# A double step of the blocked down projection written as two single steps

## The chip, the cores and the metric

One core of one Trainium2 chip runs the kernel; the other seven are idle. The metric is the device time of one execution in microseconds (us), the median of several runs. The engines are named as in the profile: PE (matmul), PEld (weight load), DVE (vector), ACT (scalar), POOL (GpSimd), SP (the queue that issues most transfers).

## What is computed

One layer of a streaming encoder, 512 positions by 1024 features, float32. Three parts come one after the other: a mixer (gated short convolution beside attention), its output projection with a residual sum, and a channel mixer with 2816 hidden features. Only the channel mixer touches the change:

```python
h = rms_norm(x, norm_ffn_g[l])
up = causal_dwconv(h @ w_up[l], conv_ffn_w[l])
a, b = jnp.split(up, 2, axis=-1)
x = x + (jax.nn.silu(a) * b) @ w_down[l]
...
return rms_norm(x, norm_f_g)
```

`silu(a) * b` is called the gated product here. It has 22 blocks of 128 features, and `w_down` has 8 output blocks of 128.

## The kernel before

**Arithmetic.** Each float32 operand is held as a rounded high part and a remainder (`wh`, `wl` for weights, `gh`, `gl` for the gated product), and each product is three matmuls: `wh*gh`, `wh*gl`, `wl*gh`.

**Steps.** The hidden blocks are worked through in two phases (`PHASES`, blocks 0 to 11 and 12 to 21). In a phase every block `j` is first projected up, convolved and gated, and then the down projection of the phase runs as a list of steps (`STEPS[ph]`, line 48). The down projection works on pairs: `(i, q)` is output pair `i` (blocks 2i, 2i+1) by hidden pair `q` (blocks 2q, 2q+1), done with seven half-size products where eight would be usual. A step holds two such `(i, q)` (a double step) or one (a single step). In phase 1 output pairs 0, 1, 2 by hidden pairs 6 to 10 are done so, and blocks 6 and 7 of the output follow plainly (`dp` chunks, `pdA` and `pdB`).

**Chunks.** A step needs two weight chunks: P (3 blocks of 128 columns for each `(i, q)`) and F (4 blocks). A double step has a P of 768 and an F of 1024 columns, with 18 and 24 matmuls; a single step has 384 and 512 columns, with 9 and 12. `split()` (line 253) turns a raw chunk into `wh` (ACT, line 275) and `wl` (DVE, line 279). `wh` and `wl` have two buffers each, so the split of a chunk can begin when PE has done with the chunk two before it. The raw P and `dp` chunks have four buffers (tag `raw`), the raw F chunks four (`rf`), filled in order by SP (line 182, `load`).

**F chunks are made on the chip.** The weight sums of F are built in DRAM by `make_forms` (line 190), for groups of up to two steps of the same size: `put` copies from SP (line 208) and accumulating `add` transfers from POOL (line 211), six for each group in the order put, add, put, add, put, add, each waiting for the one before. They are issued at `slot()` calls, two for each block `j` and one for each P chunk of the down steps: operation `k` of group `g` at slot `3k+g` in phase 1 (`GROUPS[1]`). Slots 14, 16 and 18 stand ahead of blocks 19, 20 and 21, slots 15, 17 and 19 in the middle of them, and slot 20 at the first P chunk.

**Forms of the gated product.** For each hidden pair, `glu()` (line 1230) queues the sums and differences `t13` and `t24` (lines 1256 to 1261) and four high/low splits `hl` (ACT line 1265, then DVE line 1266): `ge`, then the parts x=0, x=4 and x=2 of `go`. They become `gh` and `gl` of the seven products. Products of P read `gh`/`gl` numbers 0 (from `ge`), 1 (x=0) and 6 (x=4), in this order; those of F read 2 (x=0), 3, 4 (x=2) and 5 (x=4).

**The list `later`.** Such work isn't issued at once. It waits in `later` with a chunk number from which it is due and an estimated time; each `split()` issues what is due and fits its budget (`run_later`, 1.6 us at a P chunk and 0.75 us at an F chunk in the down steps), behind the two instructions of the split. Whatever a P or F chunk needs and is still in the list is issued ahead of that chunk's matmuls (`flush`). For the last pair of a phase the forms are due from the fourth to the sixth chunk after the gating:

```python
d = (2, 3, 4) if j + 1 < PHASES[ph][1] else (4, 5, 6)
w = [(d[0], 0.85, t13), (d[0], 0.85, t24), (d[1], 0.7, hl(ge[:, : 1 + ph, :], slice(g0, g0 + 1 + NF * ph, NF)))]
w += [(d[x > 0 and 2 or 1], 0.7, hl(go[:, x : x + 2, :], slice(g0 + 1 + x, g0 + 3 + x))) for x in (0, 4, 2)]
```

The order of matmuls on PE is that of the program, and so are the orders of the transfers on SP and POOL and of the gating products on POOL. The instructions of ACT and DVE are ordered by a planner when the program is built, which takes the earliest in the program among those ready by its own model. `seven()` (line 824) runs the steps: flush, matmuls of the chunk, then the split of the next chunk. When an output pair has had its last step, `combine()` (line 1277) queues its sums.

Of the kernel before, what the change touches and what calls it, by code (L numbers as in the profile page):

```python
# [47 lines left out]
STEPS = (  # L48
    tuple(((i, q), (i, q + 1)) for i, q in ((0, 0), (0, 2), (1, 0), (1, 2), (0, 4), (1, 4)))
    + tuple(((i, q), (i, q + 1)) for i in (3, 2) for q in (0, 2, 4)),  # L50
    (((2, 6), (2, 7)), ((2, 8), (2, 9)), ((0, 6), (0, 7)), ((0, 8), (2, 10)), ((0, 9), (0, 10)))
    + (((1, 6),), ((1, 7), (1, 8)), ((1, 9), (1, 10))),
)

# [1485 lines left out]
```

## Time and profile before

| | |
|---|---|
| median of 3 runs | 695.39 us (695.22 to 695.82) |
| the profiled execution's own time | 695.33 us |
| its span, first to last instruction | 693.5 us |
| PE busy | 682.6 us (98%) |
| DVE busy | 554.8 us (80%) |
| ACT busy | 368.5 us (53%) |
| POOL busy | 190.6 us (27%) |
| mean granted PE clock | 0.998 |

The profile is of one execution. Its page lists the busy time of each engine, the chain of work that ended last, and groups of instructions. Further views are the waits (who waited for whom), the timeline (start, duration, engine, line and operation of each instruction, with the idle time before it in brackets), stretches of time with each engine's busy time and the granted clock, and the transfers with their time to landing. Successive matmuls overlap in the records, so the time of a chunk is the distance between the starts of its first matmul and the next chunk's first.

In phase 1 of this execution the down steps begin at about 630.5 us and the plain `dp` part at 668.3 us. The steps are numbered 0 to 7 here, with their chunks P0, F0, P1 and so on; step 3 is `((0, 8), (2, 10))`.

### The profile page before, as it was taken

The numbers are of one execution on the slowest core, as the hardware profiler recorded it, in microseconds if no ns is written. First come the engines' busy times: TensorE is split into PE (matmuls) and PEld (weight loads), VectorE is DVE, ScalarE is ACT, GpSimd is POOL, SyncE is SP. The second block draws the span as 40 slices with busy tenths as digits, with TensorE's granted clock in tenths as the row PEclk, the third lists the DMA queues.
The fourth block names the chain that finished last, engine by engine and source line by source line (L and its number), as shares of the span: only waits on it lengthen the run. The fifth ranks groups of instructions, "written<-read, shape, count | busy, mean of one in ns | idle before, by whom it ended". The sixth has DMA issues, their size and how long they took to land. (4 is left out here: it accounts for less than half of the span.)

```text
span 693.5 us, 14692 instructions
## 1 busy us (share of the span) xinstructions
PE 682.6 (98%) x5936; PEld 680.4 (98%) x5936; DVE 554.8 (80%) x858; ACT 368.5 (53%) x579; POOL 190.6 (27%) x201
## 2 busy tenths in 40 slices
PE   9999999999999999999999999999999999999995
PEld 8999999999999999999999999999999999999995
DVE  6677887877577778769778799998777889987794
ACT  5665765554554444546564555546454635545572
POOL 6134947542020201214400144340100415321000
PEclk9999999999999999999999999999999999999999
DMA  8618999552668586788997498888945996576313
GB/s 310 225 68 288 219 235 215 132 116 92 193 137 225 164 276 202 231 305 208 160 306 243 127 246 212 203 215 272 244 139 174 336 243 157 160 188 182 132 31 122
DMA packets 65012, 137.53 MB, mean 198 GB/s; under 512 B 5760, under 2 KB 30352, under 8 KB 64688
## 3 DMA queue, kind: packets, MB, share of 16 engines
q1 hardware_dynamic: 44664, 107.28, 46.4%
q0 software_dynamic: 18464, 26.03, 23.7%
q10 hardware_dynamic: 1816, 3.29, 1.3%
q8 instruction: 46, 0.75, 0.5%
q14 instruction: 22, 0.18, 0.1%
HBM read 132.31 MB, written 47.71 MB: 260 GB/s over the span
## 5 line engine op out<-in xcount | busy, mean ns | idle before, releaser
L211 POOL DMA_DIRECT2D f<-in_wst_dram x66 | 77.1, 1361 | 28.1 <-DMA f<-f 27.8
L309 PE MATMUL p_up<-x1l,wh_up 128*128 128x256 f32 x416 | 81.1, 276 | 0.0
L309 PE MATMUL p_up<-x1h,wh_up 128*128 128x256 f32 x416 | 81.1, 276 | 0.0
L309 PE MATMUL p_up<-x1h,wl_up 128*128 128x256 f32 x416 | 81.0, 276 | 0.0
L279 DVE TENSOR_TENSOR wl_F<-raw_F,wh_F 128x1024 fp32r<-128x1024 f32 (+1 forms) x42 | 55.9, 1332 | 20.7 <-ACT wh_F L275 20.6
L275 ACT ACTIVATE wh_F<-raw_F 128x1024 fp32r<-128x1024 f32 (+1 forms) x42 | 44.3, 1054 | 40.9 <-PE dn L327 26.9
L309 PEld LDWEIGHTS p_up<-x1l,wh_up 128*128 128x128 f32 x416 | 62.7, 188 | 0.0
L309 PEld LDWEIGHTS p_up<-x1h,wh_up 128*128 128x128 f32 x416 | 62.6, 188 | 0.0
L309 PEld LDWEIGHTS p_up<-x1h,wl_up 128*128 128x128 f32 x416 | 62.6, 188 | 0.0
L309 PE MATMUL p_in<-xgh,wh_in 128*128 128x256 f32 x288 | 56.8, 279 | 0.0
L309 PE MATMUL p_in<-xgh,wl_in 128*128 128x256 f32 x288 | 56.6, 278 | 0.0
L309 PE MATMUL p_in<-xgl,wh_in 128*128 128x256 f32 x288 | 56.5, 278 | 0.0
L279 DVE TENSOR_TENSOR wl_P<-raw_P,wh_P 128x768 fp32r<-128x768 f32 (+1 forms) x42 | 41.7, 993 | 14.6 <-ACT wh_P L275 8.9
L275 ACT ACTIVATE wh_P<-raw_P 128x768 fp32r<-128x768 f32 (+1 forms) x42 | 35.1, 835 | 32.1 <-PE dn L327 21.8
L327 PE MATMUL dn<-gh,wh_F 128*128 128x256 f32 x216 | 51.0, 276 | 0.0
L327 PE MATMUL dn<-gl,wh_F 128*128 128x256 f32 x216 | 51.0, 276 | 0.0
L1239 POOL TENSOR_TENSOR ge<-fu,fu 128x512 f32<-128x512 f32 x11 | 20.1, 1829 | 109.6 <-DVE fu L570 76.4
L279 DVE TENSOR_TENSOR wl_up<-raw_up,wh_up 128x1024 fp32r<-128x1024 f32 x34 | 43.8, 1289 | 7.4 <-ACT wh_up L275 7.4
L275 ACT ACTIVATE wh_up<-raw_up 128x1024 fp32r<-128x1024 f32 x34 | 35.9, 1054 | 18.4 <-PE p_up L309 8.3
L309 PEld LDWEIGHTS p_in<-xgh,wh_in 128*128 128x128 f32 x288 | 44.7, 188 | 0.7
L309 PEld LDWEIGHTS p_in<-xgl,wh_in 128*128 128x128 f32 x288 | 43.7, 188 | 0.0
L309 PEld LDWEIGHTS p_in<-xgh,wl_in 128*128 128x128 f32 x288 | 43.6, 188 | 0.0
(343 smaller groups left out, 2214.1 us busy)
## 6 DMA issues: line engine op xcount, KB each, us to landing
raw_F<-f SPq DMA_DIRECT2D x41, 512.0 KB, 5.9
raw_up<-in_wup_dram SPq DMA_DIRECT2D x34, 512.0 KB, 5.4
raw_P<-in_wst_dram SPq DMA_DIRECT2D x41, 384.0 KB, 5.4
raw_in<-in_win_dram SPq DMA_DIRECT2D x24, 512.0 KB, 3.6
f<-in_wst_dram POOLq DMA_DIRECT2D x41, 256.0 KB, 7.0
f<-in_wst_dram SPq DMA_DIRECT2D x20, 512.0 KB, 7.2
f<-in_wst_dram POOLq DMA_DIRECT2D x20, 512.0 KB, 9.2
f<-f SPq DMA_DIRECT2D x40, 256.0 KB, 6.6
```

The costliest lines, as they stand in the source:

```text
L211: return lambda: keep(nc.gpsimd.dma_start(dst, src, accum_op=ALU.add))
L275: ins = nc.scalar.activation(hi, raw, AF.Copy)
L279: ins = nc.vector.tensor_sub(lo, raw, hi.bitcast(F32))
L309: keep(nc.tensor.matmul(out[:, cs], w, x[:, cs], start=start and i == 0 and c == 0, stop=stop and i == 2 and c == len(cut) - 1,))
L327: keep(nc.tensor.matmul(out, wl if x == 1 else wh, xl if x == 2 else xh, start=opens and bk not in seen, stop=closes and bk not in left,))
L1239: keep(nc.gpsimd.tensor_mul(ge, a.rearrange(halves_of, h=2), b.rearrange(halves_of, h=2)))
```

## The change

Step 3 of phase 1 is replaced by two single steps, `(0, 8)` and then `(2, 10)`:

```diff
-    (((2, 6), (2, 7)), ((2, 8), (2, 9)), ((0, 6), (0, 7)), ((0, 8), (2, 10)), ((0, 9), (0, 10)))
+    (((2, 6), (2, 7)), ((2, 8), (2, 9)), ((0, 6), (0, 7)), ((0, 8),), ((2, 10),), ((0, 9), (0, 10)))
     + (((1, 6),), ((1, 7), (1, 8)), ((1, 9), (1, 10))),
```

The list has nine steps afterwards. The new steps are called 3a, `(0, 8)`, and 3b, `(2, 10)`, here, and the others keep their old numbers. All that is derived from the list follows: the order of the products, the chunks in `stream`, the layout of the weights in `_layout`, the groups of `make_forms` (five before: steps 0 and 1, 2 and 3, 4, 5, 6 and 7; six after: 0 and 1, 2, 3a and 3b, 4, 5, 6 and 7), and the points at which `later` is worked off.

## The prediction

> **What bounds the kernel now.** I read the page's head first, then PE's waits, then the timeline of PE around the longest of them, then DVE and ACT at the same place. The page says that PE is the bound: 682.6 of 693.5 us busy, so time is only to be had where PE stands still or where something else makes it stand still.
>
> ```profile
> span 693.5 us, 14692 instructions
> ...
> PE 682.6 (98%) x5936; PEld 680.4 (98%) x5936; DVE 554.8 (80%) x858; ACT 368.5 (53%) x579; POOL 190.6 (27%) x201
> ```
>
> Among PE's waits the longest single one is for a form of the gated product, on the line of the down steps (total, times, longest):
>
> ```profile
> PE dn L327 <- DVE gl L1266: 1.4, 1, 1.4
> ```
>
> PE's timeline places it in step 3, the step that the change divides. The rows below are the first matmuls of F2, P3, the two around the wait, and the first of P4, F4, P5, F5 and P6 (start, duration).
>
> ```profile
> 642.02 0.28 PE L327 MATMUL dn<-gh,wh_F 128*128 128x256 f32 x1
> ...
> 644.74 0.28 PE L327 MATMUL dn<-gh,wh_P 128*128 128x256 f32 x1
> ...
> 645.90 0.38 PE L327 MATMUL dn<-gh,wh_P 128*128 128x256 f32 x1
> 647.65 0.39 PE L327 MATMUL dn<-gl,wh_P 128*128 128x256 f32 x1 [1.36 <-DVE gl L1266]
> ...
> 651.40 0.28 PE L327 MATMUL dn<-gh,wh_P 128*128 128x256 f32 x1
> ...
> 653.52 0.28 PE L327 MATMUL dn<-gh,wh_F 128*128 128x256 f32 x1
> ...
> 656.24 0.28 PE L327 MATMUL dn<-gh,wh_P 128*128 128x256 f32 x1
> ...
> 657.26 0.28 PE L327 MATMUL dn<-gh,wh_F 128*128 128x256 f32 x1
> ...
> 658.62 0.35 PE L327 MATMUL dn<-gh,wh_P 128*128 128x256 f32 x1
> ```
>
> F2's 24 matmuls take 644.74 - 642.02 = 2.72 us, so one takes 0.1134 us when nothing holds it up. At that pace step 3 (42 matmuls) takes 4.76 us; it takes 651.40 - 644.74 = 6.66 us. The bracket shows 1.36 us of idle time, but the step loses 1.90 us: 1.64 us between the starts of the two matmuls at the wait (1.75 less 0.11), and 0.26 us after it, where the matmuls follow each other more slowly. P4 behind it is slow as well, 653.52 - 651.40 = 2.12 us where 18 matmuls at pace are 2.04, another 0.08 us. So up to 1.98 us, 0.28% of the time, hang on this place. It isn't the granted clock: that is 1.00 in this stretch (its last three columns are clock, transfer share and GB/s).
>
> ```profile
> 644.70:648.60 3.90, 2.54 (x21) 2.28 (x21) 2.89 (x4) 1.63 (x3) 0.00 (x0) 1.00 0.39 134
> ```
>
> What PE waits for can be followed on ACT and DVE. The matmul at 647.65 is the twelfth of P3. In the order of `passes` the first twelve are `wh*gh` and `wh*gl` of six products, first three of (0, 8), then three of (2, 10), and the twelfth reads `gl` number 6 of pair 10, part x=4.
>
> ```profile
> 643.75 0.63 ACT L1265 ACTIVATE gh<-go 128x512 fp32r<-128x512 f32 x1 [0.32 <-DVE go L1260]
> 644.28 1.05 ACT L275 ACTIVATE wh_F<-raw_F 128x1024 fp32r<-128x1024 f32 x1
> 645.24 0.61 ACT L1265 ACTIVATE gh<-go 128x512 fp32r<-128x512 f32 x1
> ```
>
> ```profile
> 642.42 0.96 DVE L279 TENSOR_TENSOR wl_P<-raw_P,wh_P 128x768 fp32r<-128x768 f32 x1 [0.15 <-ACT wh_P L275]
> 643.30 0.42 DVE L1260 SCALAR_TENSOR_TENSOR go<-go 128x256 f32<-128x256 f32 x1
> ...
> 645.77 1.22 DVE L279 TENSOR_TENSOR wl_F<-raw_F,wh_F 128x1024 fp32r<-128x1024 f32 x1
> 646.91 0.69 DVE L1266 TENSOR_TENSOR gl<-go,gh 128x512 fp32r<-128x512 f32 x1
> ```
>
> The reader is to see a queue, not one slow instruction: `flush` puts three high/low splits of pair 10 ahead of P3's matmuls, the last sums that they need (`t24`) are themselves only issued with the split of P3 (643.30), and the split of F3 gets in between on both engines (644.28 and 645.77). The last form is done at 646.91 + 0.69 = 647.60, and PE goes on at 647.65.
>
> **The change part by part.**
>
> *PE.* The same 42 matmuls, in another order: P3a 9, F3a 12, P3b 9, F3b 12. The trace has one single step, step 5: P5 takes 657.26 - 656.24 = 1.02 us and F5 658.62 - 657.26 = 1.36, together 2.38, half of a double step. So the matmuls cost nothing more, 2 x 2.38 = 4.76 us.
>
> *When pair 10 is needed.* P3a and F3a read pair 8 only, whose forms are long done. With P3a starting at 644.74 as before, F3a starts at 645.76, P3b at 647.12, F3b at 648.14 and P4 at 649.50. The sixth matmul of P3b is the one that reads x=4: due at 647.12 + 5 x 0.1134 = 647.69. That is 0.09 us after the form was done even in the old order of work (647.60).
>
> *When pair 10 is ready.* Budgets are now spread over more splits: `t24` and `ge` with P3a (as before), x=0 with F3a (0.7 us of 0.75), x=4 and x=2 with P3b (1.4 of 1.6). `flush` finds nothing left at P3b. The splits are smaller; step 5 has their durations, on ACT and then on DVE:
>
> ```profile
> 653.02 0.53 ACT L275 ACTIVATE wh_P<-raw_P 128x384 fp32r<-128x384 f32 x1 [1.03 <-PE dn L327]
> 655.54 0.64 ACT L275 ACTIVATE wh_F<-raw_F 128x512 fp32r<-128x512 f32 x1 [1.99 <-PE dn L327]
> ```
>
> ```profile
> 653.98 0.55 DVE L279 TENSOR_TENSOR wl_P<-raw_P,wh_P 128x384 fp32r<-128x384 f32 x1
> ...
> 656.50 0.69 DVE L279 TENSOR_TENSOR wl_F<-raw_F,wh_F 128x512 fp32r<-128x512 f32 x1 [0.77 <-ACT wh_F L275]
> ```
>
> Laid out by hand with these, without any overlap of neighbours, and with 0.62 and 0.69 us for the two halves of a form: on ACT `wh` of F3a ends at 644.64 (it can start when F2's 16th matmul ends, 644.00), x=0 at 645.26, `wh` of P3b at 646.12 (after P3a's sixth matmul, 645.59), x=4 at 646.74, x=2 at 647.36, `wh` of F3b at 648.00. On DVE `wl` of F3a runs from 644.91 (F2's end) to 645.60, x=0 to 646.28, `wl` of P3b to 646.83, **x=4 to 647.51** (due 647.69), x=2 to 648.19 (due at F3b's fourth matmul, 648.48), `wl` of F3b to 648.88 (due at its ninth, 649.04). `wh` of F3b has 0.14 us to spare, the others 0.16 to 0.29. So the wait goes, but narrowly, and DVE is what is late next.
>
> *Cost of the pieces.* DVE works 2 x 0.55 - 0.96 + 2 x 0.69 - 1.22 = 0.30 us more, ACT 2 x 0.53 - 0.85 + 2 x 0.64 - 1.05 = 0.44 us (0.85 is the row of `wh` of P0 below). Both are in the layout above, hidden behind PE. If that cover were gone, 0.30 us of DVE would come straight off the gain. The Trainium skill, "VectorE: DVE Perf Modes", section on the TRN2 errata, speaks against the change here: each DVE or ACT instruction on SBUF pays a fixed time whatever its length, so it asks for tiles of at least 512 elements, and 384 is below. The rows agree that halves cost more than half (0.55 against 0.96); by the rule alone the change would cost, and by the rows the cost lies under PE.
>
> *Transfers.* SP issues two more weight loads and three more `put`, POOL three more `add`, for the sixth group; the bytes are the same. They fall on slots that were empty: puts on 5, 11 and 17, adds on 8, 14 and 20. The one that can hold up others is the put of slot 17. It is queued on SP behind the last `raw_up` load and ahead of the load of P0, and waits for the add of slot 14, which on POOL stands at the latest behind `ge` of block 18. Behind it on SP are the loads of P0, F0 and all later chunks.
>
> ```profile
> 601.49 0.33 SPq L182 DMA_DIRECT2D raw_up<-in_wup_dram  x1
> 609.51 0.33 SPq L182 DMA_DIRECT2D raw_P<-in_wst_dram  x1
> ```
>
> ```profile
> 603.26 3.23 POOL L1239 TENSOR_TENSOR ge<-fu,fu 128x512 f32<-128x512 f32 x1 [6.08 <-DVE fu L570]
> 606.44 1.08 POOL L211 DMA_DIRECT2D f<-in_wst_dram  x1
> ```
>
> The adds between 534 and 640 us take this long to land, and so do the P loads in the same stretch; the third row is the split of P0 on ACT:
>
> ```profile
> DMA to landing us min/median/max: 4.7/7.0/12.3
> ```
>
> ```profile
> DMA to landing us min/median/max: 2.9/4.9/9.1
> ```
>
> ```profile
> 625.22 0.85 ACT L275 ACTIVATE wh_P<-raw_P 128x768 fp32r<-128x768 f32 x1 [0.83 <-PE p_up L309]
> ```
>
> So the new add starts at about 606.4 and lands at 613.4, at worst 618.7; P0's load starts 4 to 9 us later than its 609.51 and lands at 618.3, at worst 627.8. P0's matmuls start three double steps before P3, at 644.74 - 3 x 4.76 = 630.5, and need `wh` 0.85 us earlier to begin, by 629.6. The stall on SP stays hidden, at worst by 1.8 us. I take 0 for it. An add costs POOL 1.08 us, and POOL's next product, at 614.85, was idle before it for 7.32 us: hidden as well.
>
> *Behind the steps.* From P4 on each engine has the same instructions in the same order, 1.9 us earlier. One transfer there was just in time: the second `dp` load, whose split on ACT stands in front of the split of P6.
>
> ```profile
> 649.98 4.91 SPq L182 DMA_DIRECT2D raw_dp<-in_wdp_dram  x2
> ```
>
> ```profile
> DMA to landing us min/median/max: 2.6/2.6/2.6
> ```
>
> ```profile
> 657.17 0.64 ACT L275 ACTIVATE wx<-raw_dp 128x512 fp32r<-128x512 f32 x1 [0.99 <-DMA raw_dp<-in_wdp_dram]
> 657.71 0.83 ACT L275 ACTIVATE wh_P<-raw_P 128x768 fp32r<-128x768 f32 x1
> ```
>
> It was issued at about 654.6, landed 2.6 us later, and `wh` of P6 was ready at 658.54 for a first matmul at 658.62. Any longer landing is PE's loss one for one. Afterwards the loads ahead of it are closer: F7's follows the end of `wl` of F3b (648.88) instead of F3 (646.91 + 0.08), so it and the first `dp` load overlap. Bounds: below nothing (0.15 us back, if P6 were to run at pace), and 3.2 us, if it takes the 5.8 us that is the median of the F loads between 534 and 640 us:
>
> ```profile
> DMA to landing us min/median/max: 3.2/5.8/9.1
> ```
>
> I take 0.15 us lost, near the row of this very load, since the transfer engines are busy 0.19 of the time while it is under way (last column but one):
>
> ```profile
> 654.00:656.00 2.00, 2.00 (x20) 2.00 (x19) 1.73 (x4) 0.46 (x1) 0.00 (x0) 1.00 0.19 41
> ```
>
> *Sum.* The profiled execution took 695.33 us, 1.83 outside its span of 693.5; the median of the runs is 695.39, so the two agree within 0.06 and I work from the median. 695.39 - 1.98 + 0.15 = **693.6 us**, 0.26% less.
>
> **The rivals.** *A. The forms come late again.* If the planner lets the split of F3b pass in front of x=4, as it let F3 pass in front of it before (645.77), then `wl` of F3b ends at about 648.1 to 648.2, x=4 at 648.8, and P3b stands for 1.15 us, with 0.25 behind it. That gives 695.39 - 1.98 + 1.40 = 694.8. Against it: x=4 then has its sums done 2 us earlier, so it is ready when its turn comes. The skill's rule above leans to this side.
>
> *B. The second `dp` load is somewhat late.* With 3.5 us to landing instead of 2.6 PE loses 0.9 us: 695.39 - 1.98 + 0.9 = 694.3.
>
> *C. The same load is very late, and the kernel is slower.* Place: ACT's queue at the split of P6. From a landing of 2.6 + 2.0 = 4.6 us on nothing is gained, from 6.0 us on the loss passes 0.2%. At 7.5 us, between the median and the longest of the F loads, PE stands 4.9 us: 695.39 - 1.98 + 4.9 = 698.3. For it: ACT takes its queue in order, and loads in the busier stretch do take that long. Against it: only 256 KB, and few transfers beside it.
>
> **How the numbers follow.** A measurement of this kernel can tell about 0.2%, 1.4 us, from no change, so "faster" ends at 694.0. The forecast, 693.0 to 694.0, has 0.62; A 0.14; B 0.10; C 0.14, of which 0.10 beyond 6.0 us and 0.04 between, within 0.2%. Faster is 0.62, same 0.14 + 0.10 + 0.04 = 0.28, slower 0.10. The range takes in A and B with a margin of 0.2 us, so 693.0 to 695.0. Below it lies only the case that another stall of PE happens to go too.
>
> **What would show it.** Right: no wait of PE for `gl` on line 1266 in phase 1; P3a to P4 4.8 us apart; x=4 done before P3b's sixth matmul; everything behind 1.8 to 2.0 us earlier. Wrong: a wait in P3b for `gl` or in F3b for `wh_F` (A); a wait of PE for `wh_P` behind step 5, with ACT waiting for `raw_dp` for longer than 0.99 us (B, C); a wait at P0 for `wh_P`, with SP standing at line 208 beyond 619 us. The prediction fails altogether if the planner orders ACT and DVE differently far from step 3, which the trace of before can't show.

## The result, and the profile after

The kernel after takes 692.83 us (median of 7 runs, 692.54 to 694.68), the kernel before beside it 695.55 us (694.89 to 695.84). The ratio is 0.9967 with a 95% interval of 0.9955 to 0.9978: 0.33% faster, between 1.5 and 3.1 us; the two medians lie 2.7 us apart. The median lies 0.2 us below the lower end of the range. The profiled execution of after took 692.54 us, with a span of 690.8 us against 693.5.

PE's waits in the kernel after (total, times, longest): the wait on line 1266 is gone, and what is left is elsewhere and stands in before too.

```profile
PE warm L115 <- DVE ones L107: 1.1, 1, 1.1
PE p_up L327 <- DVE wl_up L279: 0.4, 1, 0.4
PE dn L327 <- DVE wl_F L279: 0.4, 1, 0.4
```

PE's timeline of after, with the first matmuls of P3a, F3a and P3b, the sixth of P3b, and the first of F3b, P4, F4, P6 and F6:

```profile
644.63 0.28 PE L327 MATMUL dn<-gh,wh_P 128*128 128x256 f32 x1
...
645.65 0.28 PE L327 MATMUL dn<-gh,wh_F 128*128 128x256 f32 x1
...
647.01 0.28 PE L327 MATMUL dn<-gh,wh_P 128*128 128x256 f32 x1
...
647.57 0.28 PE L327 MATMUL dn<-gl,wh_P 128*128 128x256 f32 x1
...
648.03 0.28 PE L327 MATMUL dn<-gh,wh_F 128*128 128x256 f32 x1
...
649.39 0.28 PE L327 MATMUL dn<-gh,wh_P 128*128 128x256 f32 x1
...
651.43 0.28 PE L327 MATMUL dn<-gh,wh_F 128*128 128x256 f32 x1
...
656.53 0.28 PE L327 MATMUL dn<-gh,wh_P 128*128 128x256 f32 x1
...
658.57 0.28 PE L327 MATMUL dn<-gh,wh_F 128*128 128x256 f32 x1
```

The reader is to see the four chunks at full pace, 649.39 - 644.63 = 4.76 us, with no bracket of idle time. On DVE the form that was late comes as the first of a row of two, behind `wl` of P3b and ahead of `wl` of F3b:

```profile
646.09 0.55 DVE L279 TENSOR_TENSOR wl_P<-raw_P,wh_P 128x384 fp32r<-128x384 f32 x1
646.59 1.30 DVE L1266 TENSOR_TENSOR gl<-go,gh 128x512 fp32r<-128x512 f32 x2
647.80 0.68 DVE L279 TENSOR_TENSOR wl_F<-raw_F,wh_F 128x512 fp32r<-128x512 f32 x1
```

x=4 is done at about 646.59 + 0.69 = 647.28, 0.29 us before the matmul that reads it. Counted from the start of step 3, the form was done at 2.86 us in before and is done at 2.65 us in after, while its reading, after 11 matmuls at pace, would have come at 1.25 us in before and comes at 2.94 us in after. So the reading moved by 1.69 us and the form by only 0.21 us: in the change itself nearly all of the gain is the later reading.

The 2.7 us between the two profiled executions divide so, from the starts of the same chunks in both and the last output transfer that SP issues (`dp` starts at 668.29 and 666.05):

| stretch | before | after | difference |
|---|---|---|---|
| start of the span to P3 | 644.74 | 644.63 | -0.11 |
| step 3 | 6.66 | 4.76 | -1.90 |
| P4 | 2.12 | 2.04 | -0.08 |
| P6 | 2.19 | 2.04 | -0.15 |
| `dp` to the last output issue | 20.7 | 20.7 | 0 |
| from there to the end of the span | 4.5 | 4.0 | -0.5 |

Two of these were not foreseen: P6 and the end. The first row can't be put down to the change: in a second trace of after (below) P3a starts at 645.37. At P6 the planner has changed the order on ACT. In after, `wh` of P6 goes ahead of the split of the second `dp` chunk, which had stood in front of it:

```profile
655.02 0.85 ACT L275 ACTIVATE wh_P<-raw_P 128x768 fp32r<-128x768 f32 x1 [0.95 <-PE dn L327]
655.78 0.37 ACT L1285 ACTIVATE cz<-dn 128x256 f32<-128x256 f32 x1
656.04 0.62 ACT L275 ACTIVATE wx<-raw_dp 128x512 fp32r<-128x512 f32 x1
```

The end is shown by the output transfers of SP in before and in after (the last two times are the first and the last issue; the spans end at 693.5 and 690.8; with two decimals the end is 693.52 - 688.99 = 4.53 us and 690.76 - 686.73 = 4.03 us):

```profile
L1416 SPq DMA_DIRECT2D out_dram<-xm x6: 332/340/406, 680.8 to 689.0; - x6
```

```profile
L1416 SPq DMA_DIRECT2D out_dram<-xm x6: 332/341/407, 678.5 to 686.7; - x6
```

### The profile page after: what moved, and what is told of

Read it like the earlier page. It is cut to its first block, busy times and chain, and to the rows that moved or that the text cites. A ratio compares the mean times of both kernels' runs of the same rounds, so it can differ in the third digit from the quotient of the medians.

```text
span 690.8 us, 14718 instructions
## 1 busy us (share of the span) xinstructions
PE 682.3 (99%) x5936; PEld 680.6 (99%) x5936; DVE 554.6 (80%) x860; ACT 368.4 (53%) x581; POOL 192.8 (28%) x204
## 4 chain that ended last, share of the span: by engine, by line
PE 92%; DVE 5%; ACT 1%; issue 1%; POOL 0%; DVEq 0%; POOLq 0%; ACTq 0%
PE dn L327 27%; PE p_up L309 17%; PE p_in L309 14%; PE p_wo L309 6%; PE p_up L327 5%; PE yc L309 3%; PE ya L309 3%; PE pa L477 2%; PE pb L479 2%; PE p_q L309 2%; PE p_k L309 2%; PE o L658 2%; PE tp L641 1%; DVE wl_up L279 1%; PE pdB L309 1%; PE pdA L309 1%
## 5 line engine op out<-in xcount | busy, mean ns | idle before, releaser
L211 POOL DMA_DIRECT2D f<-in_wst_dram x69 | 79.7, 1341 | 26.6 <-DMA f<-f 26.2
```

The source lines that it names most:

```text
L211: return lambda: keep(nc.gpsimd.dma_start(dst, src, accum_op=ALU.add))
```

## The experiments

Theory W: the gain is the wait for the forms of pair 10, which goes because they are read later. Rival S: the smaller splits free ACT and DVE, wherever pair 10 stands. Rival R: the transfers, or the planner's new order. Three groups of kernels ran on three chips, each beside the kernel before (695.4, 695.58 and 695.72 us there).

**The new half first.**

```diff
-((0, 8),), ((2, 10),)
+((2, 10),), ((0, 8),)
```

> The two single steps exchanged: (2, 10), with the new forms, ahead of (0, 8). Theory W (PE gains because pair 10 is needed later): P3a now needs x=4 at its sixth matmul, about 0.6 us into the step, while the three high/low splits are flushed in front of it; x=4 is done 0.45 to 1.1 us too late, so a wait of PE for line 1266 is back and the time is 694.3 to 694.9. Rival S (the smaller splits get ACT and DVE out of the way sooner, whichever half comes first): no wait, 693.4 or less.

693.73 us, ratio 0.9970 (0.9960 to 0.9980). The wait is back, as W has it and S has not, on the sixth matmul of the new first chunk:

```profile
646.59 0.39 PE L327 MATMUL dn<-gl,wh_P 128*128 128x256 f32 x1 [0.50 <-DVE gl L1266]
```

That chunk takes 647.17 - 645.36 = 1.81 us instead of 1.02, so 0.79 us are lost, within the 0.45 to 1.1 expected. The time is lower than expected because P6 runs at pace and the end is shorter here too (4.0 us), which I had not counted. The order of the halves is worth about 0.8 us of the gain. The rest stays because the form is done sooner here, 646.54 - 645.36 = 1.18 us into its step where before has 2.86. On DVE no split of an F chunk gets ahead of it; the third of the three forms below is x=4:

```profile
644.65 1.89 DVE L1266 TENSOR_TENSOR gl<-go,gh 128x512 fp32r<-128x512 f32 x3
646.46 0.69 DVE L279 TENSOR_TENSOR wl_F<-raw_F,wh_F 128x512 fp32r<-128x512 f32 x1
```

How much of that comes from the smaller pieces (S) and how much from the order on DVE this run doesn't separate.

**Forms earlier, step undivided.**

```diff
-else (4, 5, 6)
+else (4, 5, 6) if not ph else (3, 4, 5)
```

> Kernel before, its step undivided; only the forms of the last pair of phase 1 are due one chunk earlier, from the third to the fifth chunk. W: x=4 is done before the twelfth matmul of P3, the wait of 1.36 us goes, 693.2 to 693.6. S: with the large splits the wait stays, 695.5.

693.53 us, ratio 0.9969 (0.9958 to 0.9979). No wait of PE for line 1266 is left, and step 3 takes 649.44 - 644.68 = 4.76 us with its large splits. So the wait alone makes up 1.9 us of the profiles' difference, and the division isn't needed to remove it. The median is 0.7 us above that of after, but that comes from another group of runs, and the ratios to before (0.9969 and 0.9967) don't tell the two kernels apart. The profiles do differ by 0.7 us (spans of 691.5 and 690.8), at the other two places. ACT still waits for the `dp` chunk ahead of P6 (which takes 2.18 us and starts 0.09 late), and 4.5 us lie behind the last output issue:

```profile
655.25 0.63 ACT L275 ACTIVATE wx<-raw_dp 128x512 fp32r<-128x512 f32 x1 [1.13 <-DMA raw_dp<-in_wdp_dram]
655.79 0.83 ACT L275 ACTIVATE wh_P<-raw_P 128x768 fp32r<-128x768 f32 x1
```

**Another step divided.** Step 4 as `((0, 9),), ((0, 10),)`, step 3 double:

```diff
-((0, 8), (2, 10)), ((0, 9), (0, 10)))
+((0, 8), (2, 10)), ((0, 9),), ((0, 10),))
```

> Kernel before with the step after it, ((0, 9), (0, 10)), divided instead, where PE waits for nothing; five groups of forms as before. It prices two more chunks alone. W: the wait of 1.36 us at P3 stays and the pieces are hidden, 695.4 to 695.8. S: smaller splits help wherever they are, under 695. If the fixed cost of each piece comes through: up to 0.3 us slower, 695.8.

694.72 us, ratio 0.9988 (0.9978 to 0.9997). The wait of 1.36 us is still there, against S. The time is lower than W had it, but not in the steps: from P3 to `dp` they take 668.75 - 644.80 = 23.95 us, where before took 668.29 - 644.74 = 23.55, and the kernel with its groups cut anew below, with its steps undivided, 23.42. The gain is all at the end, 3.3 us behind the last output issue instead of 4.5. In the steps time is lost here: F4b and F5 take 1.70 and 1.73 us instead of 1.36. At F4b the sums of output pair 2 stand ahead of the small split on DVE:

```profile
653.95 0.68 DVE L1297 TENSOR_TENSOR xm<-xm,dn 128x512 f32<-128x512 f32 x1
654.55 0.68 DVE L1300 TENSOR_TENSOR xm<-xm,cz 128x512 f32<-128x512 f32 x1
655.15 0.68 DVE L279 TENSOR_TENSOR wl_F<-raw_F,wh_F 128x512 fp32r<-128x512 f32 x1
```

`wl` is ready at 655.83, and the ninth matmul of F4b, a chunk that starts at 654.77, wanted it at 655.68. At F5 it is the sums of output pair 0, which ends with step 4 (lines 1286 and 1289, up to 657.99), that stand ahead of the split. How much of the loss is the fixed cost of the added pieces isn't separated from this queue. In this place, where DVE has sums to do, the divided step was not free.

**Order within the chunk.** The matmuls of P3 and F3 in two halves, (0, 8) first:

```diff
-            passes(out, len(out))
+            for m in (out[: len(out) // 2], out[len(out) // 2 :]) if d_late(doubles, n) else (out,):
+                passes(m, len(m))
```

> Kernel before, its step undivided; only the matmuls of P3 and of F3 are put in two halves, all nine (twelve) of (0, 8) ahead of those of (2, 10). W: x=4 is read at the fifteenth matmul instead of the twelfth, 0.34 us later, so the wait shrinks from 1.36 to about 1.0 us and the time to about 695.2. S: no change, 695.5. If order within the chunk were all that counts: 693.5.

694.85 us, ratio 0.9991 (0.9980 to 1.0002), which doesn't tell it from no change; the trace does, though its execution was a long one (696.71 us, with time lost ahead of the steps). P3 takes 650.53 - 647.03 = 3.50 us, so it loses 1.46, where P3 of the kernel with its groups cut anew loses 1.79: 0.33 us better, as three matmuls are worth. The bracket is the one in this kernel's PE timeline:

```profile
649.94 0.39 PE L327 MATMUL dn<-gl,wh_P 128*128 128x256 f32 x1 [1.16 <-DVE gl L1270]
```

**The form x=4 done twice, in the kernel after.**

```diff
-                nc.vector.tensor_sub(gl[:, gs, :], src, gh.bitcast(F32)[:, gs, :])
+                for _ in range(2 if gs.start == place(1, 10) + 5 else 1):
+                    nc.vector.tensor_sub(gl[:, gs, :], src, gh.bitcast(F32)[:, gs, :])
```

> Kernel after, with the DVE half of the high/low split x=4 of pair 10 done twice (the second writes the same values). It takes 0.6 us more just ahead of the matmul that reads it. In the trace of after that form is done at about 647.3 and read at 647.57. W: P3b waits about 0.3 us, with up to 0.26 us of slow matmuls behind it: 693.1 to 693.4. Rival (the division left wide room there): no wait, 692.8.

694.00 us, ratio 0.9973 (0.9961 to 0.9986), 1.2 us over the median of after, which was measured in another group of runs. PE waits 0.80 us instead of the 0.3 expected, and P3b takes 649.40 - 647.31 = 2.09 us instead of 1.02:

```profile
648.84 0.38 PE L327 MATMUL dn<-gl,wh_P 128*128 128x256 f32 x1 [0.80 <-DVE gl L1267]
```

```profile
646.89 1.90 DVE L1267 TENSOR_TENSOR gl<-go,gh 128x512 fp32r<-128x512 f32 x3
648.70 0.68 DVE L279 TENSOR_TENSOR wl_F<-raw_F,wh_F 128x512 fp32r<-128x512 f32 x1
```

Three forms run in a row ahead of `wl` of F3b, and PE goes on right after the third, at 646.89 + 1.90 = 648.79: so the second copy seems to stand behind x=2 as well, and two instructions came in the way, about 1.2 us, not one. It was wanted at 647.31 + 0.57 = 647.88, so 1.2 us more on DVE made it 0.91 late: the room was 0.29 us, what the trace of after shows. P3b's gain hangs on that much.

**Groups of forms cut anew, steps undivided.**

```diff
-len(DOUBLES[n]) != len(DOUBLES[cuts[-1]]):
+len(DOUBLES[n]) != len(DOUBLES[cuts[-1]]) or n == ND[1] + 3:
```

> Kernel before, all steps double as they were; only the groups of forms are six instead of five (steps 2 and 3 each a group of their own), so that the six added transfers and their slots are there without the division. W: the wait of 1.36 us stays, 695.5. Rival R (part of the gain comes from the transfers or from the planner's new order behind them): under 695.

695.63 us, ratio 1.0002 (0.9987 to 1.0017), and the wait is there (1.36 us, at 647.50). But this kernel isn't what the expectation says. It cuts behind step 2, and steps 3 and 4, which are both double, then make a group together: 0 and 1, 2, 3 and 4, 5, 6 and 7, five groups as before. No transfer is added. The accumulating transfers on POOL are 15 in this kernel, as many as in before, and 18 in after:

```profile
L211 POOL DMA_DIRECT2D f<-in_wst_dram x15: 831/1332/2204, 541.0 to 628.0; - x15
```

```profile
L211 POOL DMA_DIRECT2D f<-in_wst_dram x18: 830/1096/1984, 541.4 to 628.5; - x18
```

So no run has the six added transfers without the division. Against their part in R stand other runs: the wait goes in the second experiment with the transfers of before, and in both traces of after, which has them, every chunk from P0 to F7 runs at pace. The other side of R, the planner's order, does hold for P6 (0.15 us, told below). What this run does give is the undivided step a second time: P3 to P4 651.16 - 644.59 = 6.57 us, P4 2.04. So the wait costs 1.81 us (the trace with step 4 divided gives 1.82), and the slow matmuls of F3 and P4 in the one execution of before (about 0.17 us) do not belong to it.

**Double steps, older forms first.**

```diff
-((0, 8), (2, 10)), ((0, 9), (0, 10)))
+((0, 8), (0, 9)), ((2, 10), (0, 10)))
```

> All steps stay double; the halves are paired anew: ((0, 8), (0, 9)) and then ((2, 10), (0, 10)), so pair 10 is read a whole step later. W: the wait at P3 goes (2.0 us), but output pair 2 now ends right ahead of step 5, which opens the same four banks, so PE waits there for the sums of combine, 2 to 3 us: 695.5 to 696.5. S: the wait at P3 stays, over 697.

699.50 us, ratio 1.0052 (1.0038 to 1.0066). P3 runs at pace (2.04 us), as W has it, and the wait that takes its place at step 5 is longer than I expected:

```profile
658.19 0.38 PE L327 MATMUL dn<-gh,wh_P 128*128 128x256 f32 x1 [3.71 <-DVE cz L1286]
```

Reading the pair later removes the wait for its forms, but with whole steps it pushes the end of output pair 2 against step 5, which needs its banks. Two output pairs end together there, and on DVE the sums of pair 0 are in the way of those of pair 2. The halves keep the end of pair 2 one step away from step 5.

**The kernel after, forms earlier as well** (the edit of the second experiment on the kernel after), on two chips, the second time beside after itself:

> Kernel after with the forms of pair 10 due one chunk earlier as well. W: there is no wait left for them, so no change: 692.6 to 693.0. If the division left a hidden loss at P3b or F3b: up to 0.3 us faster.

> Kernel after with the forms of pair 10 one chunk earlier, again, now beside after on one chip. W: no difference from after beyond 0.3 us, since no wait for forms is left. If a hidden loss was left: up to 0.3 us faster than after.

> Kernel after, unchanged, beside the others on one chip: 692.6 to 693.0.

693.12 us, ratio 0.9955 (0.9939 to 0.9970); then 693.04 us, ratio 0.9958 (0.9943 to 0.9973), beside after at 692.77 us, ratio 0.9955 (0.9938 to 0.9971). No difference beyond 0.3 us between two medians of four runs each: nothing more is to be had from these forms, and no kernel here is measurably faster than after.

**The end of the kernel.** Behind the last output issue there are 4.5 us in before and in the second, sixth and seventh experiments, 4.3 in the fourth, but 3.8 to 4.0 in every kernel with step 3 divided and 3.3 with step 4 divided. The trace shows 8 KB fetches of instructions there (queue q14). In the last 3.5 us of before and of after, the view of transfers lists under this queue one and none; this is the row of before:

```profile
q14 instruction: 1, 0.01, 0.9%
```

To see whether the number of instructions decides, four tiny ones were put in, without the division:

```diff
+    for _ in range(2):
+        nc.vector.tensor_copy(tbl, ones[: 4 * H, :1])
+    for _ in range(2):
+        nc.scalar.activation(tbl, ones[: 4 * H, :1], AF.Copy)
```

> Kernel before, undivided, with four tiny instructions more (two on DVE, two on ACT, on a 32x1 tile that nothing reads) long before the steps, as many as the division adds on these engines. Theory T: the 0.4 us that after gains behind its last output transfer come from the number of instructions ahead, since a late fetch of instructions that all undivided kernels show there is gone; then the end shortens here as well, from 4.5 us behind the last output issue to about 4.0, and the time is 694.9 to 695.1, with the wait of 1.36 us still there. Rival: the end has to do with the division or with chance, 695.4.

> The forms of pair 10 one chunk earlier in the undivided kernel, and the four tiny instructions. W and T together: both gains without the division, 693.0 to 693.2, within 0.3 us of after. Rival: the division itself is worth something, over 693.5.

696.14 us, ratio 1.0011 (1.0001 to 1.0021), and 694.58 us, ratio 0.9977 (0.9968 to 0.9987): both expectations of the time missed. The end did shorten, to 3.9 us in both. But a new wait of PE appeared at 54.5 us, in the projections, some 10 us behind the four instructions (42.5 to 44.1 us); the kernels without them do not have it. The row is of the first of the two:

```profile
PE p_in L309 <- DVE wl_in L279: 1.4, 1, 1.4
```

So the length of the end changes without the division, by instructions that do no work. But it isn't the same part of it. The end has two parts in the records of transfers, from the last output issue to the last packet of data and from there to the end of the span:

| kernel | to the last packet | from there on |
|---|---|---|
| before | 2.3 | 2.2 |
| after | 2.3 | 1.7 |
| step 4 divided | 1.9 | 1.5 |
| four tiny instructions (both) | 1.9 | 2.0 |

What after gains is in the second part; the tiny instructions shorten mostly the first. They don't bear theory T out, and the cause of the shorter end stays open: these two kernels still fetch instructions 0.3 us before the end, before does so 0.5 us before it and the one with step 4 divided 1.4 us before it. That the fetches set the length is not shown.

## Why the prediction was right, and where its sum was off

- **What bounds.** Right. The one wait in step 3 was the matter, and its cause the queue of forms and splits: moving the forms one chunk earlier removes it with the steps undivided (1.9 us), doing the form twice in after brings it back.
- **"Up to 1.98 us hang on this place."** Nearly. Step 3 gave 1.90 us in the two profiles, and 1.81 against the second trace of the undivided step. The 0.08 us of P4 and a part of the 0.26 us were in that one execution only.
- **When pair 10 is needed and ready.** Right: due at 647.57, 0.12 us earlier than laid out, done at 647.28, 0.23 us earlier; 0.11 us of each is that P3a itself started earlier. The room was put at 0.18 us and is 0.29, in the trace of after and again when the form is done twice. The layout without overlap was about 0.1 us slow.
- **Cost of the pieces.** Right here: hidden. With step 4 divided two chunks take 1.70 and 1.73 us where 1.36 would do, at a place where DVE is already the later engine; how much of this is the added pieces isn't separated from the sums queued there. The rule that the Trainium skill has on this ("VectorE: DVE Perf Modes", TRN2 errata) names the cost of each instruction; whether it reaches the time depends on the place, as these two divisions show.
- **Transfers.** Nothing lost, as forecast, as far as the traces of after show: all chunks from P0 on at pace. No run has the transfers alone. The stall of SP that I bounded didn't come: the add of slot 14 stands ahead of `ge` of block 18 on POOL, not behind it, so the new put went out 1.4 us behind the last `raw_up` load and P0's load kept its time:

```profile
596.95 1.05 POOL L211 DMA_DIRECT2D f<-in_wst_dram  x1
603.06 3.23 POOL L1239 TENSOR_TENSOR ge<-fu,fu 128x512 f32<-128x512 f32 x1 [5.06 <-DVE fu L570]
```

```profile
601.29 0.33 SPq L182 DMA_DIRECT2D raw_up<-in_wup_dram  x1
602.68 0.47 SPq L208 DMA_DIRECT2D f<-f  x1
609.29 0.33 SPq L182 DMA_DIRECT2D raw_P<-in_wst_dram  x1
```

- **Behind the steps.** This failed: "From P4 on each engine has the same instructions in the same order". The planner put the split of the second `dp` chunk behind that of P6. I took 0.15 us lost there, and 0.15 us were won, the lower bound that I had given. It is the order that counts, not the division: P6 takes 2.16 to 2.22 us in the five traces with the old order, and 2.04 in the fourth experiment, where the step is undivided and the planner put the split of P6 first. Rivals B and C rest on the old order and fell with it. Where that order stays with step 3 freed of its wait, in the second experiment, the load landed 655.23 - 652.61 = 2.6 us after its issue, as in before.
- **The end.** A term that the sum lacked: 0.5 us behind the last output issue, its cause open. With P6 (0.15 us won instead of lost) it is what puts the median 0.2 us under the range. The wait, worth 1.81 to 1.90 us instead of the 1.98 taken, went the other way.
- **Rival A** did not come: the planner kept x=4 ahead of `wl` of F3b.

## What to carry to other kernels

When an engine waits at a chunk for freshly made operands, look for the half of the chunk that doesn't need them and what may run between; but try first to have the operands made earlier, which here gave most of the gain with no more pieces. A finer step paid here only where the engine that feeds it had room, and a reordering must be checked at the next place that needs the same buffers, where the one with whole steps lost more than the wait (699.5 us). In a list ordered by a planner, a local edit can also change the order several chunks away: a term of some tenths of a microsecond on either side belongs in every such sum.

## What the runs showed beside this

Behind the issue of the last output transfer the program ran on for 3.3 to 4.5 us, by kernel; both the transfer (1.9 to 2.4 us to its last packet) and what follows it (1.5 to 2.2 us) varied. And matmuls of the same form followed each other at 0.1134 us, or at 0.118 us through whole chunks (F3 and P4 of before, and P6 of before after a first step of 0.19 us), with a granted clock of 1.00 in each: here a busy PE ran 4% slower without any wait being listed. Why isn't shown.
